# Planner priorities for weight splits and norms, and gamma folded into the opening's split

## The chip, the cores and the metric

The kernel runs on one NeuronCore of one Trainium2 chip. The metric is the device time of one execution in microseconds (us). Engines are named as in the profile: PE is the matmul engine, PEld its weight loads, DVE the vector engine, ACT the scalar engine, POOL is GpSimd, SP issues most DMAs.

## The reference, cut to what matters

Two layers work on x, 256 tokens by 1024 channels, all in float32. Cut to the parts that the change touches:

```python
for l in range(DEPTH):                               # DEPTH = 2
    h = rmsnorm(x, norm_mix[l])
    aq, ak, av, iq, ik, iw, hq, hf, hi, hg, ga, gb = split(h @ w_in[l])   # D_IN = 5956 columns
    y_attn = dsa_attention(aq, ak, av, iq, ik, iw)   # indexer scores, top 64 keys, softmax
    y_hgrn = hgrn2(hq, hf, hi) * silu(hg)            # gated linear recurrence
    merged = sigmoid(ga) * (y_attn @ w_proj_attn[l]) + sigmoid(gb) * (y_hgrn @ w_proj_hgrn[l])
    x = x + merged @ w_out[l]
    h = rmsnorm(x, norm_ffn[l])
    g, u = split(h @ w_ffn_in[l])
    x = x + (silu(g) * u) @ w_ffn_out[l]
```

## The kernel before, in words

**Arithmetic.** Each float32 matmul is made of three matmuls in the fp32r type: an operand is split into a rounded part `hi` and the rest `lo`, and `mm3` adds hi\*hi, hi\*lo and lo\*hi into one PSUM bank. Activations are the stationary side (128x128), weights the moving side (up to 512 columns). Tokens come in NT = 2 tiles of 128 (index `i`).

**Weights.** `take()` brings the next chunk of weights: SP issues the DMA into a tile `w`, ACT writes `hi` (a rounded copy), DVE writes `lo = w - hi`. There are three slots each for `hi` and `lo`. A usual chunk has 128x2048 elements and feeds 24 pairs or more of matmul and weight load; the eight chunks of the first layer's `idx` and `aq` are smaller (128x648 and 128x1024), because those groups are cut in four. `group()` runs one column group over all chunks and both token tiles; the order of groups in a layer is idx, aq, ak, hf, hq, av, vh, hg, then the gates ga, gb, ga, gb. After these come pj (the two projections), wo, fi (feed-forward in) and fo (feed-forward out). The accumulators of groups lie in four PSUM banks with tag `P`, transposes and small products in four with tag `Q`.

**Between the matmuls.** The indexer result goes through ropes and the top-64 search (`work`: pairs of MAX8 and MATCH_REPLACE8 on DVE), aq and ak through a norm and ropes, then softmax; hf and hq are copied out by ACT (`hfraw`, `hqraw`), transposed on PE (`hfp`, `hqp`) and go into the recurrence. Temporaries of these steps share six slots with tag `s2`.

**Order.** Nothing is ordered by hand. Every operation is recorded in a `Program`, and a planner (`schedule`, `path_tails`, `run`) fixes the order on each engine before anything is emitted. An operation has a cost in planner nanoseconds and a `tail`: the longest way from its start to the end, along what needs its result, along the chain of all matmul groups that are marked main, and along who reuses its slots (that hop costs `slack` more). The cost of an operation that is neither main nor on SP is multiplied by `stretch` in that sum, so work beside PE is treated as more urgent than its bare length says. On each engine the planner takes, of the operations that could start first, the one with the largest `tail + rank`. `rank` is a number in nanoseconds that the kernel may set around some operations.

```python
    def path_tails(self, stretch, slack):
        for o in reversed(self.ops):
            after = [s.tail + self.latency(o, s) for s in o.succs] + [s.tail + slack for s in o.soft]
            if o in self.next_main:
                after.append(self.next_main[o].tail)
            o.tail = (o.cost if o.main or o.eng == "SP" else o.cost * stretch) + max(after, default=0.0)
```

**The opening.** 28 small bfloat16 matmuls on zeros (`gate`, WARM of them) have a rank of -1e9 and fill PE while nothing else can run. The four blocks of x (two token tiles by two halves of 512 channels) are loaded, transposed on PE into a bank `xT`, multiplied by the norm weight gamma on DVE into `xg` (gamma lies by channel in `gcol`), rounded by ACT to `hT_hi`, and `hT_lo = xg - hT_hi` is made by DVE for the first block and by POOL for the other three.

**Norms at the end of a block.** `out_gemm` (wo and fo) finishes its two token tiles and two halves one after another; each half is added into x by DVE, multiplied by gamma, transposed, and split (`norm_half`).

All operations go through one recorded call, so nearly every row of the profile has the line L467; rows are told apart by the names of the tiles.

Of the kernel before, what the change touches and what calls it, by code (L numbers as in the profile page):

```python
# [9 lines left out]
F32 = mybir.dt.float32  # L10
# [3 lines left out]
AF = mybir.ActivationFunctionType  # L14
ALU = mybir.AluOpType
# [11 lines left out]
N_IDX = 324  # L27
C_HQ, C_HF, C_HV, C_HG, C_GA, C_GB = 1860, 2372, 2884, 3396, 3908, 4932
FIRST = {(0, C_IDX): 2, (0, C_AQ): 2}
WARM = 28  # L30
LEVELS = (2, 4, 8)
TWO_PI = 2.0 * np.pi

# [120 lines left out]
class Program:  # L154
# [298 lines left out]
    def emit(self, tc):  # L453
        nc = tc.nc
        engines = {"DVE": nc.vector, "ACT": nc.scalar, "PE": nc.tensor, "SP": nc.sync, "POOL": nc.gpsimd}
        with ExitStack() as ctx:
# [15 lines left out]
BASE, ORIGIN = 16512, 24576  # L472
SLOTS = {"w": 3, "hi": 3, "lo": 3, "hT": 8, "s4": 14, "s2": 6, "sm": 14, "work": 2, "bias": 2, "rqs": 4,
         "gbc": 2, "P": 4, "Q": 4}
TUNING = {"stretch": 1.5, "bonus": 3000.0, "slack": 4000.0}


def hybrid_trunk(prog, x_d, pos_d, w_in, w_pa, w_ph, w_out, n_mix, n_ffn,
                 q_norm, k_norm, h_norm, h_lb, w_fi, w_fo, invf_d, cf_d, cm_d, out_d):
    V, S, PE, SP, POOL = prog.vector, prog.scalar, prog.tensor, prog.sync, prog.gpsimd  # L480

    def const(name, shape, dt=F32):
        prog.add_tag("c_" + name, 1)
        return prog.tile("c_" + name, shape, dt, name)
# [4 lines left out]
    def tmp(name, shape, dt=F32):  # L489
        return prog.tile("s2", shape, dt, name)  # L490
# [4 lines left out]
    def bank(name, tag="Q"):  # L495
        return prog.tile(tag, [512], F32, name)
# [21 lines left out]
                                     for o in (0, DFF)]) + ([4, 512],))  # L518
        add_rows(w_fo, l, 2, 1024, 0)

    state = {"used": 0}

    def take():
        c = state["used"]
        state["used"] += 1
        a, b, kn = chunks[c]
        k, n = kn or b
        wt, ht, lt = "w" if k * n > 1024 else "s4", "hi", "lo"
        w = prog.tile(wt, [k, n], F32, f"w{c}")
        hi = prog.tile(ht, [k, n], F32R, f"hi{c}")  # L530
        lo = prog.tile(lt, [k, n], F32R, f"lo{c}")
        prog.rank = 5e5 - 1e3 * c
        if kn is None:
            SP.dma_start(w, a)
        else:
            SP.dma_start(w[:, :, 0:256], a)
            SP.dma_start(w[:, :, 256:512], b)
        prog.rank = 0.0
        S.activation(hi, w, AF.Copy)
        V.tensor_tensor(lo, w, hi.bitcast(F32), op=ALU.subtract)  # L540
        return hi, lo

    def mm3(acc, h, hk, wc, wk, wsl, start, stop):

        hh, hl = h
        wh, wl = wc
        with prog.one(main=True):
            PE.matmul(acc, hh[:, hk, :], wh[:, wk, wsl], start=start, stop=False)
            PE.matmul(acc, hh[:, hk, :], wl[:, wk, wsl], start=False, stop=False)
            PE.matmul(acc, hl[:, hk, :], wh[:, wk, wsl], start=False, stop=stop)  # L550
# [19 lines left out]
    V.memset(zero, 0.0)  # L570
    prog.rank = 2e6
    grow = tmp("grow", [128])
    S.dma_start(ident, cf_d[:, 0:128])
    S.dma_start(grow[0:8, :], n_mix[0].rearrange("(k d) -> k d", k=8))
    for g in range(2):
        for i in range(NT):
            prog.rank = (2e6, 499500.0)[g + i > 0] - 1e3 * (2 * g + i - 1)
            gs = slice(g * 512, (g + 1) * 512)
            SP.dma_start(x[:, i, gs], x_d[0, i * 128:(i + 1) * 128, gs])
    prog.rank = 0.0  # L580
# [2 lines left out]
    gate = bank("gate")  # L583
    for _ in range(WARM):
        PE.matmul(gate[:, 0:256], zero[:, 0:128], zero, start=True, stop=True)
# [24 lines left out]
    def transpose4(dst, src, n=4):  # L610
        with prog.one():
            for k in range(n):
                PE.transpose(dst[:, k * 128:(k + 1) * 128], src[:, k * 128:(k + 1) * 128], ident)
# [26 lines left out]
    gcol = const("gcol", [8])  # L640
    V.tensor_copy(gcol, growp[:, 0:8])
    hT = pair("hT0")
    for g in range(2):
        ks = slice(g * 4, g * 4 + 4)
        for i in range(NT):
            pt = bank(f"xT{i}{g}", "P")
            transpose4(pt, x[:, i, g * 512:(g + 1) * 512])
            xg = tmp(f"xg{i}{g}", [4, 128])
            V.tensor_tensor(xg, pt.rearrange("p (k t) -> p k t", k=4), gcol[:, ks, None].to_broadcast([128, 4, 128]), op=ALU.mult)
            first_hi = S.activation(hT[i][0][:, ks, :], xg, AF.Copy)  # L650
            E = V if g == 0 and i == 0 else POOL
            E.tensor_tensor(hT[i][1][:, ks, :], xg, hT[i][0][:, ks, :].bitcast(F32), op=ALU.subtract)
    R = []
    for i in range(NT):
        ssq = small(f"ss{i}")
# [97 lines left out]
    def layer(l, hT, R):  # L753
        last = l == DEPTH - 1
        def group(n, name, evac, kk=4):
            accs = [bank(f"{name}{i}_{l}", "P") for i in range(NT)]
            for c in range(8 // kk):
                wc = take()
                for i in range(NT):
                    for k in range(kk):  # L760
                        kt = c * kk + k
                        mm3(accs[i][:, :n], hT[i], kt, wc, k, slice(0, n), kt == 0, kt == 7)
            for i in range(NT):
                evac(i, accs[i][:, :n])
# [52 lines left out]
        def ev_qk(a, dstT):  # L817
            def ev(i, acc):
                raw = tmp(f"raw{a}{i}", [512])
                S.activation(raw, acc, AF.Copy, scale=R[i][:, 0:1])  # L820
                sq = tmp(f"sq{a}{i}", [512])
                S.activation(sq, raw, AF.Square)
                s8 = small(f"s8{a}{i}")
                V.tensor_reduce(s8[:, 0:8], sq.rearrange("p (h d) -> p h d", h=8), axis=AX.X, op=ALU.add)
                r8 = newton(s8[:, 0:8], 8, 1.0 / 64, f"n{a}{i}")
                rot = tmp(f"rot{a}{i}", [8, 64])
                rope(rot, raw.rearrange("p (h d) -> p h d", h=8), 8, rtab[l, a][0][:, i, :], rtab[l, a][1][:, i, :])
                if a == 0:
                    rqs = prog.tile("rqs", [8], F32, f"rqs{i}")
                    V.tensor_scalar(rqs, r8, 0.125, None, op0=ALU.mult)  # L830
                    rq.append(rqs)
                else:
                    V.tensor_tensor(rot, rot, r8[:, :, None].to_broadcast([128, 8, 64]), op=ALU.mult)
                pt = bank(f"qkp{a}{i}")
                transpose4(pt, rot.rearrange("p h d -> p (h d)"))
                S.activation(dstT[:, :, i * 128:(i + 1) * 128], pt.rearrange("p (k t) -> p k t", k=4), AF.Copy)
            return ev

        group(512, "aq", ev_qk(0, qT), FIRST.get((l, C_AQ), 4))
        load_g(f"f{l}", n_ffn[l])  # L840
        group(512, "ak", ev_qk(1, kT))


        PT = []
        for i in range(NT):
# [17 lines left out]
            for p in range(2):  # L863
# [4 lines left out]
                for hp in range(4):  # L868
                    h, c = 2 * hp + p, p * 4 + hp
# [4 lines left out]
                for j in range(i + 1):  # L874
                    pt = bank(f"ptp{i}{p}{j}")
# [178 lines left out]
        for i in range(NT):  # L1054
# [10 lines left out]
            pt = bank(f"yhp{i}")  # L1065
# [3 lines left out]
            split_to(yT[i][0][:, 4:8, :], yT[i][1][:, 4:8, :], pv, gc)  # L1069


        gates = {}

        def ev_gate(key):
# [11 lines left out]
        for g in range(2):  # L1086
            ws = [take(), take()]
            for i in range(NT):
# [10 lines left out]
                pt = bank(f"mp{i}", "Q")  # L1099
# [3 lines left out]
        def out_gemm(n_chunks, lhs, gkey, hT_out, name):  # L1103

            accs = [[bank(f"{name}{i}{g}", "Q") for g in range(2)] for i in range(NT)]
            for c in range(n_chunks - 2):
                wc = take()
                for i in range(NT):
                    for k in range(2):
                        (hh, hl), hk = lhs(i, 2 * c + k)  # L1110
                        with prog.one(main=True):
                            for g in range(2):
                                gs = slice(g * 512, (g + 1) * 512)
                                PE.matmul(accs[i][g], hh[:, hk, :], wc[0][:, k, gs], start=c == 0 and k == 0, stop=False)
                                PE.matmul(accs[i][g], hh[:, hk, :], wc[1][:, k, gs], start=False, stop=False)
                            for g in range(2):
                                gs = slice(g * 512, (g + 1) * 512)
                                PE.matmul(accs[i][g], hl[:, hk, :], wc[0][:, k, gs], start=False, stop=False)
            wcs = [take(), take()]
            Rn = []  # L1120
            for i in range(NT):
                ssq = small(f"{name}ss{i}")
                for g in range(2):
                    for c in range(2):
                        for k in range(2):
                            kt = 2 * (n_chunks - 2 + c) + k
                            h, hk = lhs(i, kt)
                            mm3(accs[i][g], h, hk, wcs[c], k, slice(g * 512, (g + 1) * 512), kt == 0, c == 1 and k == 1)
                    xs = x[:, i, g * 512:(g + 1) * 512]
                    V.tensor_tensor(xs, xs, accs[i][g], op=ALU.add)  # L1130
                    if hT_out is not None:
                        norm_half(i, g, gkey, hT_out, ssq, "P")
                    else:
                        SP.dma_start(out_d[0, i * 128:(i + 1) * 128, g * 512:(g + 1) * 512], xs)
                if hT_out is not None:
                    Rn.append(norm_scale(ssq, f"{name}r{i}"))
            return Rn
# [8 lines left out]
        for j in range(11):  # L1146
# [7 lines left out]
            for i in range(NT):  # L1154
                pt = bank(f"fp{j}{i}", "Q")
# [11 lines left out]
    for l in range(DEPTH):  # L1167
        hT, R = layer(l, hT, R)
# [43 lines left out]
```

## Time and profile before

| what | us |
|---|---|
| median of 3 runs | 814.75 (814.44 to 815.56) |
| the profiled execution | 815.19 |
| its span, first to last instruction | 813.4 |
| PE busy | 801.3 |
| DVE busy | 537.6 |
| ACT busy | 400.9 |
| POOL busy | 6.5 |

The profiled execution lies 0.44 us over the median; 1.8 us of it lie around the span. PE's busy time counts the drawn-out ends of pipelined matmuls, so a matmul of 512 columns is drawn with some 0.39 us although the next one starts 0.23 us after it. A stall on PE is therefore read best from the starts of two neighbouring matmuls.

### The profile page before, as it was taken

The page shows a single profiled execution, that of the slowest core. Times are in us where ns is not written, and L with a number is a line of the kernel's source. Part 1 is how long each engine was busy: PE and PEld are TensorE (multiplying, and loading weights), DVE is VectorE, ACT ScalarE, POOL GpSimd, SP SyncE. Part 2 cuts the span into 40 slices and gives each one's busy share as a digit, 9 for nine tenths or more (in the row PEclk, how much of TensorE's full clock was granted, in tenths as well). Part 3 has the DMA queues.
Part 4 walks back from the last instruction along what each step waited for, and adds up shares of the span by engine and source line. Part 5 has one row for each costly group of instructions (what it writes and reads, how often), then busy time and mean ns, then how long its engine had stood idle before and what let it go on. Part 6 is the DMA issues. An engine that isn't in the chain of part 4 may idle for free.

```text
span 813.4 us, 10251 instructions
## 1 busy us (share of the span) xinstructions
PE 801.3 (99%) x3986; PEld 657.3 (81%) x3986; DVE 537.6 (66%) x936; ACT 400.9 (49%) x506; POOL 6.5 (1%) x8
## 2 busy tenths in 40 slices
PE   8989999999999999999999999999999999999998
PEld 7767788888888888888887778888888888888886
DVE  6999856577775455554489997566868645556442
ACT  5764855344364435453356667533445544445330
POOL 3000000000000000000000000000000000000000
PEclk9998999999999999999999999999999999999999
DMA  9725555333656656536546356443354665655531
GB/s 319 248 69 176 186 188 174 104 124 129 219 176 206 195 169 203 170 144 222 168 154 219 111 201 207 155 156 105 108 202 156 206 204 168 199 177 186 169 142 52
DMA packets 86793, 139.66 MB, mean 172 GB/s; under 512 B 3269, under 2 KB 51033, under 8 KB 86745
## 3 DMA queue, kind: packets, MB, share of 16 engines
q1 hardware_dynamic: 86584, 138.94, 51.4%
q8 instruction: 31, 0.51, 0.2%
q14 instruction: 18, 0.14, 0.0%
q10 hardware_dynamic: 160, 0.07, 0.0%
HBM read 137.95 MB, written 1.05 MB: 171 GB/s over the span
## 4 chain that ended last, share of the span: by engine, by line
PE 84%; DVE 10%; issue 2%; ACT 2%; DMA 0%; POOL 0%; POOLq 0%; ACTq 0%; DVEq 0%
PE fi L467 29%; PE fo L467 15%; PE pj L467 5%; PE gb L467 5%; PE wo L467 5%; PE ga L467 4%; DVE lo L467 4%; PE av L467 3%; PE hg L467 3%; PE vh L467 3%; PE hq L467 2%; DVE work L467 2%; PE aq L467 1%; ACT hi L467 1%; PE fp L467 1%
## 5 line engine op out<-in xcount | busy, mean ns | idle before, releaser
L467 DVE TENSOR_TENSOR lo<-w,hi 128x2048 fp32r<-128x2048 f32 (+3 forms) x134 | 296.4, 2212 | 218.5 <-ACT hi L467 217.9
L467 ACT ACTIVATE hi<-w 128x2048 fp32r<-128x2048 f32 (+3 forms) x134 | 247.3, 1846 | 280.7 <-PE fi L467 95.1
L467 PE MATMUL fi<-hi,h2T_hi 128*128 128x512 f32 x352 | 140.8, 400 | 0.2
L467 PE MATMUL fi<-hi,h2T_lo 128*128 128x512 f32 x352 | 137.8, 391 | 0.0
L467 PE MATMUL fi<-lo,h2T_hi 128*128 128x512 f32 x352 | 137.1, 390 | 0.0
L467 PE MATMUL fo<-hi,act 128*128 128x512 f32 x352 | 109.9, 391 | 0.0
L467 PEld LDWEIGHTS fi<-hi,h2T_lo 128*128 128x128 f32 x352 | 66.1, 188 | 15.0 <-DVE h2T_lo L467 0.7
L467 PEld LDWEIGHTS fo<-hi,act 128*128 128x128 f32 x352 | 66.1, 188 | 13.7
L467 PEld LDWEIGHTS fi<-hi,h2T_hi 128*128 128x128 f32 x352 | 66.1, 188 | 13.3 <-DVE h2T_lo L467 0.8
L467 PEld LDWEIGHTS fi<-lo,h2T_hi 128*128 128x128 f32 x352 | 66.2, 188 | 12.6
L467 PE MATMUL fo<-lo,act 128*128 128x512 f32 x176 | 68.5, 389 | 0.0
L467 PEld LDWEIGHTS fo<-lo,act 128*128 128x128 f32 x176 | 33.1, 188 | 6.6
L467 PE MATMUL gb<-hi,hT_hi 128*128 128x512 f32 x64 | 26.7, 418 | 0.0
L467 PE MATMUL wo<-hi,mT_hi 128*128 128x512 f32 x64 | 25.9, 405 | 0.0
L467 PE MATMUL pj<-hi,yT_hi 128*128 128x512 f32 x64 | 25.8, 404 | 0.0
L467 PE MATMUL ga<-hi,hT_hi 128*128 128x512 f32 x64 | 25.7, 401 | 0.0
L467 PE MATMUL wo<-lo,mT_hi 128*128 128x512 f32 x64 | 25.1, 392 | 0.0
L467 PE MATMUL gb<-hi,hT_lo 128*128 128x512 f32 x64 | 25.1, 392 | 0.0
L467 PE MATMUL gb<-lo,hT_hi 128*128 128x512 f32 x64 | 25.0, 391 | 0.0
L467 PE MATMUL ga<-hi,hT_lo 128*128 128x512 f32 x64 | 25.0, 391 | 0.0
L467 PE MATMUL pj<-hi,yT_lo 128*128 128x512 f32 x64 | 25.0, 391 | 0.0
L467 PE MATMUL pj<-lo,yT_hi 128*128 128x512 f32 x64 | 25.0, 390 | 0.0
(340 smaller groups left out, 1302.0 us busy)
## 6 DMA issues: line engine op xcount, KB each, us to landing
w<-in_w_ffn_in_dram SPq DMA_DIRECT2D x88, 512.0 KB, 4.5
w<-in_w_in_dram SPq DMA_DIRECT2D x42, 1024.0 KB, 4.9
w<-in_w_ffn_out_dram SPq DMA_DIRECT2D x22, 1024.0 KB, 4.7
w<-in_w_out_dram SPq DMA_DIRECT2D x8, 1024.0 KB, 4.7
w<-in_w_proj_attn_dram SPq DMA_DIRECT2D x4, 1024.0 KB, 4.9
w<-in_w_proj_hgrn_dram SPq DMA_DIRECT2D x4, 1024.0 KB, 4.8
w<-in_w_in_dram SPq DMA_DIRECT2D x4, 512.0 KB, 4.6
w<-in_w_in_dram SPq DMA_DIRECT2D x4, 324.0 KB, 5.5
```

What stands on the lines that cost most here:

```text
L467: getattr(engines[o.eng], name)(*[real(x) for x in a], **{n: real(x) for n, x in k.items()})
```

## The change

Five edits. Two constants of the planner: WARM goes from 28 to 22 and `stretch` from 1.5 to 1.8. The hi and lo of a chunk get a rank: the first four chunks (idx of the first layer) one of some 3e5, interleaved with the splits of x; chunks taken from the point after the group ak to the point after hg (the groups hf, hq, av, vh, hg, in both layers) get AHEAD = 2e4; the others stay at 0. In `out_gemm` the addition into x and `norm_half` get AHEAD as well. In the opening the multiplication by gamma is part of the split: per k tile of 128 channels one ACT instruction writes `hT_hi` from PSUM with gamma as its scale, and one DVE instruction writes `hT_lo`; `xg` and POOL's part are gone. The DMA of gamma is issued ahead of that of the identity, and the ranks of the last three blocks of x fall by LATER = 6e3, so that they stand behind more of the first weight chunks on SP's queue.

```diff
-WARM = 28
+WARM = 22
+AHEAD, LATER, OPEN = 2e4, 6e3, 3e5
-TUNING = {"stretch": 1.5, "bonus": 3000.0, "slack": 4000.0}
+TUNING = {"stretch": 1.8, "bonus": 3000.0, "slack": 4000.0}
-    state = {"used": 0}
+    state = {"used": 0, "ahead": 0.0}
...
-        prog.rank = 0.0
+        prog.rank = OPEN - 1e4 * c - 5e3 if c < 4 else state["ahead"]
         S.activation(hi, w, AF.Copy)
         V.tensor_tensor(lo, w, hi.bitcast(F32), op=ALU.subtract)
+        prog.rank = 0.0
...
+    S.dma_start(grow[0:8, :], n_mix[0].rearrange("(k d) -> k d", k=8))
     S.dma_start(ident, cf_d[:, 0:128])
-    S.dma_start(grow[0:8, :], n_mix[0].rearrange("(k d) -> k d", k=8))
...
-            prog.rank = (2e6, 499500.0)[g + i > 0] - 1e3 * (2 * g + i - 1)
+            prog.rank = 2e6 if g + i == 0 else 5e5 - 1e3 * (2 * g + i - 1) - LATER
...
             pt = bank(f"xT{i}{g}", "P")
+            prog.rank = OPEN - 1e4 * (2 * g + i)
             transpose4(pt, x[:, i, g * 512:(g + 1) * 512])
-            xg = tmp(f"xg{i}{g}", [4, 128])
-            V.tensor_tensor(xg, pt.rearrange("p (k t) -> p k t", k=4), gcol[:, ks, None].to_broadcast([128, 4, 128]), op=ALU.mult)
-            first_hi = S.activation(hT[i][0][:, ks, :], xg, AF.Copy)
-            E = V if g == 0 and i == 0 else POOL
-            E.tensor_tensor(hT[i][1][:, ks, :], xg, hT[i][0][:, ks, :].bitcast(F32), op=ALU.subtract)
+            for k in range(g * 4, g * 4 + 4):
+                src = pt[:, k % 4 * 128:k % 4 * 128 + 128]
+                first_hi = S.activation(hT[i][0][:, k, :], src, AF.Copy, scale=gcol[:, k:k + 1])
+                V.scalar_tensor_tensor(hT[i][1][:, k, :], src, gcol[:, k:k + 1], hT[i][0][:, k, :].bitcast(F32),
+                                       op0=ALU.mult, op1=ALU.subtract)
+    prog.rank = 0.0
...
         group(512, "ak", ev_qk(1, kT))
+        state["ahead"] = AHEAD
...
+        state["ahead"] = 0.0
         gates = {}
...
+                    prog.rank = AHEAD
                     xs = x[:, i, g * 512:(g + 1) * 512]
                     V.tensor_tensor(xs, xs, accs[i][g], op=ALU.add)
                     if hT_out is not None:
                         norm_half(i, g, gkey, hT_out, ssq, "P")
                     else:
                         SP.dma_start(out_d[0, i * 128:(i + 1) * 128, g * 512:(g + 1) * 512], xs)
+                    prog.rank = 0.0
```

## Rows read from the trace of the kernel before

**Rows 1.** The page, part 1: engine, busy us, share of the span, xinstructions.

```profile
PE 801.3 (99%) x3986; PEld 657.3 (81%) x3986; DVE 537.6 (66%) x936; ACT 400.9 (49%) x506; POOL 6.5 (1%) x8
```

**Rows 2.** Busy time by stretch: length, PE, PEld, DVE, ACT, POOL, clock, DMA.

```profile
0.00:20.00 20.00, 17.03 (x102) 14.22 (x103) 12.58 (x25) 12.15 (x21) 6.52 (x8) 1.00 0.90 318
...
16.00:30.00 14.00, 13.84 (x67) 11.31 (x66) 13.58 (x65) 10.66 (x14) 0.29 (x1) 1.00 0.81 292
45.00:58.00 13.00, 10.84 (x52) 8.31 (x50) 13.00 (x51) 7.45 (x9) 0.00 (x0) 1.00 0.25 81
59.70:66.50 6.80, 6.18 (x15) 4.83 (x16) 6.80 (x34) 1.78 (x4) 0.00 (x0) 0.50 0.47 154
450.00:470.00 20.00, 19.50 (x94) 15.25 (x94) 20.00 (x73) 12.65 (x14) 0.00 (x0) 1.00 0.47 156
```

**Rows 3.** Waits of PE: us in total, times, longest us.

```profile
PE hq L467 <- DVE lo L467: 1.7, 3, 1.3
PE idx L467 <- POOL hT_lo L467: 1.1, 2, 0.7
```

**Rows 4.** Timeline of PE, 55 to 67 us: start us, duration us, instruction.

```profile
55.18 0.39 PE L467 MATMUL hf<-hi,hT_lo 128*128 128x512 f32 x1
55.41 0.60 PE L467 MATMUL hfp<-ident,hfraw 128*128 128x128 f32 x4
58.16 0.66 PE L467 MATMUL hfp<-ident,hfraw 128*128 128x128 f32 x4 [2.14 <-ACT hfraw L467]
58.57 0.47 PE L467 MATMUL hq<-hi,hT_hi 128*128 128x512 f32 x1
60.32 0.79 PE L467 MATMUL hq<-lo,hT_hi 128*128 128x512 f32 x1 [1.28 <-DVE lo L467]
...
66.46 0.44 PE L467 MATMUL hq<-hi,hT_hi 128*128 128x512 f32 x1
```

**Rows 5.** Timeline of DVE, 46 to 61 us, the two lo of the stretch.

```profile
46.91 2.27 DVE L467 TENSOR_TENSOR lo<-w,hi 128x2048 fp32r<-128x2048 f32 x1
...
57.98 2.29 DVE L467 TENSOR_TENSOR lo<-w,hi 128x2048 fp32r<-128x2048 f32 x1
```

**Rows 6.** Timeline of ACT, 43 to 59 us, two instructions.

```profile
43.25 1.92 ACT L467 ACTIVATE hi<-w 128x2048 fp32r<-128x2048 f32 x1 [0.76 <-PE ak L467]
...
57.43 0.67 ACT L467 ACTIVATE hfraw<-hf,r1y 128x512 f32<-128x512 f32 x1
```

**Rows 7.** Timeline of PE, second layer, 465 to 466 us.

```profile
465.12 0.48 PE L467 MATMUL hq<-hi,hT_hi 128*128 128x512 f32 x1
465.87 0.50 PE L467 MATMUL hq<-lo,hT_hi 128*128 128x512 f32 x1 [0.26 <-DVE lo L467]
```

**Rows 8.** Timeline of PE, opening: the first idx matmul, and ak.

```profile
8.27 0.39 PE L467 MATMUL idx<-hi,hT_hi 128*128 128x324 f32 x1
...
26.00 0.48 PE L467 MATMUL ak<-hi,hT_hi 128*128 128x512 f32 x1
26.64 0.51 PE L467 MATMUL ak<-lo,hT_hi 128*128 128x512 f32 x1 [0.16 <-DVE lo L467]
```

**Rows 9.** Timeline of DVE, opening: two lo of idx chunks, and xg.

```profile
8.47 1.63 DVE L467 TENSOR_TENSOR lo<-w,hi 128x648 fp32r<-128x648 f32 x1 [0.20 <-ACT hi L467]
10.02 1.27 DVE L467 TENSOR_TENSOR xg<-xT,gcol 128x512 f32<-128x512 f32 x2
11.22 0.82 DVE L467 TENSOR_TENSOR lo<-w,hi 128x648 fp32r<-128x648 f32 x1
```

**Rows 10.** Groups by shape: xcount, busy us, mean ns, then idle before.

```profile
L467 ACT ACTIVATE hsq<-po 128x128 f32<-128x128 f32 x16 | 4.2, 278 | 4.2 <-PE po L467 4.2
L467 DVE SCALAR_TENSOR_TENSOR yh<-po,hn0y,sg 128x128 f32<-128x128 f32 x4 | 1.1, 344 | 0.0
```

**Rows 11.** Timeline of PE, first feed-forward matmuls of the first layer.

```profile
229.15 0.50 PE L467 MATMUL fi<-hi,h2T_lo 128*128 128x512 f32 x1
229.74 0.50 PE L467 MATMUL fi<-hi,h2T_hi 128*128 128x512 f32 x1
```

More of the change, by code (lines that the diff above doesn't have):

```diff
@@ L643, in hybrid_trunk @@
     for g in range(2):
-        ks = slice(g * 4, g * 4 + 4)
         for i in range(NT):
             pt = bank(f"xT{i}{g}", "P")
+            prog.rank = OPEN - 1e4 * (2 * g + i)
             transpose4(pt, x[:, i, g * 512:(g + 1) * 512])
-            xg = tmp(f"xg{i}{g}", [4, 128])
-            V.tensor_tensor(xg, pt.rearrange("p (k t) -> p k t", k=4), gcol[:, ks, None].to_broadcast([128, 4, 128]), op=ALU.mult)
-            first_hi = S.activation(hT[i][0][:, ks, :], xg, AF.Copy)
-            E = V if g == 0 and i == 0 else POOL
-            E.tensor_tensor(hT[i][1][:, ks, :], xg, hT[i][0][:, ks, :].bitcast(F32), op=ALU.subtract)
+            for k in range(g * 4, g * 4 + 4):
[4 more added lines that the diff above has]
+    prog.rank = 0.0
     R = []
```

## The prediction, on record before the changed kernel was run

> **What bounds the kernel now.** I read the page's first part first: PE is busy 801.3 of 813.4 us [rows 1], so a change of order alone can win only what PE idles or runs slowly; it removes no matmul of the main chain. The next view is the starts of PE's instructions, since drawn ends hide stalls. Two neighbouring 512-column matmuls start 0.23 us apart (55.18 to 55.41) and four transposes take (0.60 - 0.27) / 3 = 0.11 us each [rows 4]. Measured against these paces, one place stands out, the passage from hf to hq in the first layer. The transposes hfp start at 55.41, the second four only at 58.16; hq's first matmul starts at 58.57, its second at 60.32, waiting for a lo [rows 4]. After that the granted clock is 0.50 from 59.7 to 66.5 us, the lower of the two levels, 1.2 GHz [rows 2]: PE had done little for 5 us, and then pays double for each matmul until it is back.
>
> Why is that lo late? The windows show DVE with 13.00 of 13.00 us busy [rows 2]. Its hi came from ACT at 43.25 + 1.92 = 45.2 us [rows 6], but the lo ran from 57.98 to 60.27 [rows 5]: nearly 13 us behind ropes, norms and the top-64 search. So it is an order on a full DVE, not a late DMA and not a lack of DVE over the whole kernel, of which it is busy for 66% [rows 1]. The second layer has the same passage with a smaller wait [rows 3, 7]. PE's list of waits has none for a lo of the gates, the projections or the feed-forward, so there no order of splits can win.
>
> **The change, part by part.** *Splits of hf to hg at AHEAD.* Raised by 20 us of planner time, the lo of hq can follow its hi: at 45.2 instead of 57.98. PE then goes on from hf to hq, and hq's matmuls also cover the late copy hfraw (ACT, 57.43 to 58.10 [rows 6]), because the second transposes can come after some of them. From 55.41 to 66.46 pass 11.05 us, with 8 transposes and 15 matmuls (hq at 58.57 and 14 from 60.32 on; the window's x15 counts the one at 66.46 for that at 58.57 [rows 2, 4]). At the full pace that is 8 x 0.11 + 15 x 0.23 = 4.3 us, so 6.7 us go: 2.3 before 58.16, 1.5 before 60.32, and 2.9 of slow clock. The bounds are 3.8 (idle gone, the clock still falls) and 6.7; I take 6.7, since with no idle there nothing is left that is like what came before the fall. In the second layer the three waits of hq for lo sum to 1.7 with a longest of 1.3 [rows 3], which leaves 0.4 for two; by starts one of them is 465.87 - 465.12 - 0.23 = 0.5 [rows 7]. Bounds 0.4 and 1.0; I take 0.9.
>
> What is behind the moved lo on DVE? At most three of 2.29 us run earlier, so ropes, norms and search come 6.9 us later. Next late are the six s2 slots, and through them hfraw, whose copy must empty a P bank before av's matmuls. Before, hfraw is out at 58.1; 6.9 later is 65.0. PE would now reach av at 55.4 + 0.9 + 48 x 0.23 = 67.3. The cover is 2.3 us, so I price this at zero; without cover it is the second rival. SP's loads profit, as w tiles come free with their lo. The two matching hi on ACT pass copies of accumulators by 1.9 us each, covered by the 11 us between a group's end and the reuse of its bank.
>
> *The opening.* Removed are four xg (1.27 for two [rows 9], 2.5 in all) and one lo on DVE, some 0.7 more, and three subtractions on POOL, for which PE waited 1.1 us [rows 3]. Added are 16 scalar_tensor_tensor on DVE. The nearest row, four of 128x128 from PSUM with a column scalar, takes 1.1 us [rows 10]: 4.4 in all, so DVE gains 1.2 us of work. It gets most of that back: the lo at 8.47 took 1.63 us beside POOL's subtraction, the one at 11.22 0.82 [rows 9]. ACT gets 16 pieces in place of four 512-wide ones; at the 278 ns of the nearest row, without a scale, that is 4.4 us [rows 10], and with 7.8 of the first 20 us idle on ACT [rows 2] even half as much again is covered, on its idle and not on the path.
>
> Cutting 512-wide operations in four is what the Trainium skill warns of (VectorE: DVE Perf Modes, "The TRN2 errata — SBUF-src ops pay a fixed extra latency per instruction"): each instruction pays a fixed latency, so pieces should have at least 512 elements. Its table, 120 cycles plus the width at 0.96 GHz from PSUM, makes an estimate of 16 x 0.26 = 4.1 us where the row makes 4.4. By the page DVE would lose 0.9 us here, by the row 1.2.
>
> What it wins is latency. The first idx matmul, at 8.27 [rows 8], need no longer wait for a whole 512-wide product, hi and lo (some 0.64 each, as xg [rows 9]), only for two pieces of 0.28: up to 1.3 us. With POOL's 1.1 the upper bound is a gain of 2.4. The lower bound is a loss: SP now issues early weights ahead of x's last blocks; a 512 KB chunk at 292 GB/s [rows 2] is 1.8 us, and if idx waits for x that long, it is lost. What is won must also survive the next splits: DVE is busy 13.58 of 14 us from 16 to 30, and the lo of ak is just in time, or 26.64 - 26.00 - 0.23 = 0.4 late [rows 2, 8]. I take a gain of 0.8, a third of the upper bound, for that reason. Six fewer warm-up matmuls and gamma's DMA ahead of the identity's I price at nothing: the first ones still run while x loads, and the rest only fill. The opening's range pays if they don't.
>
> *Norms at AHEAD.* PE waits 229.74 - 229.15 - 0.23 = 0.36 us for h2T_lo [rows 11], once in each layer: bounds 0 and 0.7, taken 0.4, since add, transposes and split must still follow one another.
>
> *Stretch 1.8.* It lifts all work beside PE against the splits that get no rank: aq, ak, gates, feed-forward. Where PE never waits for a lo I charge nothing; the cover there is the three slots of hi and lo, which let a split run two chunks ahead, some 11 us of matmuls. In the opening, aq and ak have next to none; the nearest row is the 0.4 of ak [rows 8], and I charge that once more, a loss of 0.4; bounds are 0 and one whole lo, 2.3.
>
> Sum: 6.7 + 0.9 + 0.8 + 0.4 - 0.4 = 8.4 us. The profiled execution's span goes from 813.4 to 805.0 and its time from 815.19 to 806.8; the median, 0.44 lower, to 806.3.
>
> **The rivals.** *The rank doesn't reach.* Stretch goes up by 0.3 of a helper's cost, so a chain with 20 / 0.3 = 67 us of work beside PE still ahead of it rises as much as the splits do, and the order stays. For it: search, softmax and recurrence are long. Against it: the lo lost by 13 us only, and the matmuls in between count unstretched. The two hq terms fall away, and 0.8 remains: 814.0.
>
> *The wait moves (slower).* The delayed ropes hold s2 slots, hfraw comes after 67.3, and PE waits for a P bank at av. It decides when the copies slip by more than the 9.2 us from 58.1 to 67.3 (the 6.9 above plus 2.3). Then an idle of up to 4.6 us, as much as two lo, and the clock's 2.9 come back: 7.5 in each layer, where DVE is as full (20.00 of 20.00 [rows 2]). Layer one: 7.5 - 6.7 = 0.8; layer two: 7.5 - 0.9 = 6.6; with 0.8 won elsewhere, 814.75 + 6.6 = 821.4. For it: six slots, a DVE without gaps. Against it: the cover.
>
> *The opening loses.* x comes 1.8 us late and one lo of aq or ak slips by 2.3 more, in place of a net gain of 0.4: 806.3 + 4.5 = 810.8. For it: the loads are the limit there. Against it: idx can work on the first token tile meanwhile.
>
> **How the numbers follow.** The forecast has 0.66 (803.5 to 809.5: all terms at their upper ends give 814.75 - 6.7 - 1.0 - 2.4 - 0.7 = 804.0, half a us is for smaller stalls; the upper end is the clock's 2.9 not won), the opening's loss 0.12, the rank that doesn't reach 0.12, the moved wait 0.10. The range 803.5 to 814.0 holds the first two and the better part of the third. Within 0.2%, 813.1 to 816.4, is what measurement can't tell from no change: 0.12. Faster is 0.78, slower 0.10.
>
> **What would show it.** Right: no idle of PE between hf and hq, the clock at 1.00 from 55 to 70 us, the lo of hq on DVE right after its hi, search and ropes later; the wait for POOL gone and the first idx matmul before 8.27. Wrong: a gap of PE before av with hfraw as its releaser, a lo of aq or ak that PE waits for by over 1 us, or lo of hq still behind the search.

## The result, and the profile after

The changed kernel takes 804.39 us (median of 4 runs, 803.62 to 804.76) against 814.88 for the kernel before beside it: ratio 0.9869, interval 0.9852 to 0.9886, a gain of 10.5 us. Forecast were 806.3 in 803.5 to 814.0. The profiled execution took 804.76 us, its span is 803.0.

Part 1 of the page after, beside [rows 1]:

```profile
PE 796.7 (99%) x3980; PEld 656.7 (82%) x3980; DVE 537.6 (67%) x947; ACT 407.6 (51%) x522; POOL 0.7 (0%) x5
```

DVE does as much as before, ACT 6.7 us more, POOL next to nothing. The first table to make is where PE stood at the same point of its program. The starts are read from PE's timeline in both kernels:

| stretch of PE's program | before | after | difference |
|---|---|---|---|
| start to the first hf of layer 0 | 43.05 | 43.42 | +0.38 |
| hf to pj, layer 0 | 132.15 | 124.56 | -7.59 |
| pj of layer 0 to hf of layer 1 | 271.15 | 270.52 | -0.63 |
| hf to pj, layer 1 | 126.15 | 123.91 | -2.24 |
| pj of layer 1 to the end | 240.90 | 240.56 | -0.34 |

So most came from the passages that the prediction named, and the opening gave nothing in this profiled execution. Busy time by stretch after (length, PE, PEld, DVE, ACT, POOL, clock, DMA), to lay beside [rows 2]:

```profile
43.00:55.00 12.00, 12.00 (x56) 9.94 (x55) 11.88 (x38) 5.86 (x7) 0.00 (x0) 1.00 0.43 145
55.00:70.00 15.00, 14.94 (x68) 12.07 (x67) 15.00 (x46) 8.70 (x8) 0.00 (x0) 1.00 0.63 208
59.70:66.50 6.80, 6.80 (x33) 5.61 (x33) 6.80 (x20) 3.12 (x4) 0.00 (x0) 1.00 0.48 154
```

From 59.7 to 66.5 us PE now starts 33 instructions at a granted clock of 1.00, where it started 15 at 0.50. DVE is as full as it was; only its order changed. The waits of PE after (total, times, longest), beside [rows 3]:

```profile
PE gate L468 <- DVE zero L468: 1.1, 1, 1.1
PE xT L468 <- DMA ident<-in_cf_dram: 0.5, 1, 0.5
PE aq L468 <- DVE lo L468: 0.4, 1, 0.4
PE idx L468 <- DVE lo L468: 0.3, 1, 0.3
```

The wait of hq for lo and that of idx for POOL are gone. So are those of fi (read by starts, [rows 11]) and of the recurrence, whose product hl waited twice in the kernel before:

```profile
PE hl L467 <- DVE A L467: 0.7, 2, 0.4
```

The passage from hf to hq in PE's timeline after, beside [rows 4]:

```profile
54.55 0.39 PE L468 MATMUL hf<-hi,hT_lo 128*128 128x512 f32 x1
54.77 0.39 PE L468 MATMUL hq<-hi,hT_hi 128*128 128x512 f32 x1
55.00 0.39 PE L468 MATMUL hq<-lo,hT_hi 128*128 128x512 f32 x1
```

hq follows hf 0.22 us later, and the transposes hfp have moved behind hq, to 89.6 us. The split that made it possible, in the timelines of ACT and DVE after, beside [rows 5, 6]:

```profile
43.62 1.92 ACT L468 ACTIVATE hi<-w 128x2048 fp32r<-128x2048 f32 x1 [0.32 <-PE ak L468]
...
45.57 2.29 DVE L468 TENSOR_TENSOR lo<-w,hi 128x2048 fp32r<-128x2048 f32 x1
...
51.53 2.29 DVE L468 TENSOR_TENSOR lo<-w,hi 128x2048 fp32r<-128x2048 f32 x1
```

The hi ends at 45.54 and its lo starts at 45.57, in the middle of the search; before, a lo in the same place came 13 us behind its hi.

### The profile page after: what moved, and what is told of

Same layout as the page of the kernel before. It is cut to its first block, busy times and chain, and to the rows that moved or that the text cites. A ratio compares the mean times of both kernels' runs of the same rounds, so it can differ in the third digit from the quotient of the medians.

```text
span 803.0 us, 10263 instructions
## 1 busy us (share of the span) xinstructions
PE 796.7 (99%) x3980; PEld 656.7 (82%) x3980; DVE 537.6 (67%) x947; ACT 407.6 (51%) x522; POOL 0.7 (0%) x5
## 4 chain that ended last, share of the span: by engine, by line
PE 94%; DVE 3%; DMA 2%; ACT 0%; issue 0%; SPq 0%
PE fi L468 30%; PE fo L468 15%; PE gb L468 6%; PE ga L468 5%; PE wo L468 5%; PE pj L468 5%; PE ak L468 3%; PE vh L468 3%; PE hg L468 3%; PE aq L468 3%; PE av L468 2%; PE hf L468 1%; PE hq L468 1%; DVE lo L468 1%; PE hl L468 1%; DMA w<-in_w_in_dram 1%
## 5 line engine op out<-in xcount | busy, mean ns | idle before, releaser
L468 PE MATMUL ga<-lo,hT_hi 128*128 128x512 f32 x64 | 25.0, 391 | 0.0
```

Source lines behind the costliest of these rows:

```text
L468: getattr(engines[o.eng], name)(*[real(x) for x in a], **{n: real(x) for n, x in k.items()})
```

## The experiments

All twelve kernels ran five rounds beside the kernel before. The differences are in us against the changed kernel's 804.39, which was measured in another sitting: the kernel before stood at 814.88 beside it and at 814.78 to 815.02 beside these twelve, so a difference of 0.2 says nothing.

| kernel | median (range) | ratio to before, interval | difference |
|---|---|---|---|
| e1, splits without rank | 809.73 (808.63 to 809.99) | 0.9934 [0.9921, 0.9946] | +5.34 |
| e2, rank on splits alone | 807.48 (807.36 to 808.18) | 0.9911 [0.9898, 0.9925] | +3.09 |
| e3, stretch 1.5 | 805.42 (805.06 to 805.50) | 0.9883 [0.9868, 0.9898] | +1.03 |
| e4, old opening | 805.24 (804.96 to 805.70) | 0.9883 [0.9869, 0.9896] | +0.85 |
| e5, rank from the start | 803.38 (803.26 to 803.49) | 0.9857 [0.9842, 0.9872] | -1.01 |
| e6, five s2 slots | 807.06 (806.04 to 807.54) | 0.9902 [0.9885, 0.9918] | +2.67 |
| e7, norms without rank | 805.76 (805.42 to 806.34) | 0.9887 [0.9872, 0.9902] | +1.37 |
| e8, x not behind weights | 804.46 (804.21 to 804.52) | 0.9870 [0.9855, 0.9885] | +0.07 |
| e9, stretch alone | 815.13 (814.54 to 815.85) | 1.0000 [0.9991, 1.0009] | +10.74 |
| e10, PE kept busy | 815.66 (815.17 to 816.74) | 1.0010 [1.0001, 1.0019] | +11.27 |
| e11, e5 and LATER 0 | 804.17 (803.90 to 804.42) | 0.9867 [0.9853, 0.9880] | -0.22 |
| e12, e5 and WARM 48 | 813.60 (813.33 to 816.81) | 0.9993 [0.9984, 1.0002] | +9.21 |

**The rank of the splits, taken away and given alone.** e1 is the changed kernel without the line that sets the rank behind ak:

```diff
         group(512, "ak", ev_qk(1, kT))
-        state["ahead"] = AHEAD
```

> The changed kernel, only that the chunks of hf to hg have rank 0 again (stretch 1.8, the new opening and the rank on norms stay). If the rank on splits carries the gain, the lo of hq falls behind the search again, and further than before since stretch 1.8 lifts the search: PE idles between hf and hq by 3.8 us or more in the first layer, the granted clock falls to 0.50 there, and the time is 811 to 816 us. If stretch 1.8 carries it (helpers done earlier leave DVE free for lo), PE has no such gap and the time stays at 804 to 806.

It lies between the two expectations, at 809.73. Rows of its PE timeline, and a window:

```profile
50.98 0.63 PE L468 MATMUL qkp<-ident,rot 128*128 128x128 f32 x4 [1.65 <-DVE rot L468]
...
53.48 0.50 PE L468 MATMUL hf<-lo,hT_hi 128*128 128x512 f32 x1 [1.65 <-DVE lo L468]
...
61.07 0.50 PE L468 MATMUL hq<-lo,hT_hi 128*128 128x512 f32 x1 [1.39 <-DVE lo L468]
```

```profile
55.00:70.00 15.00, 13.62 (x75) 10.63 (x74) 15.00 (x65) 8.88 (x10) 0.00 (x0) 1.00 0.40 137
```

By starts (each row's start less that of the matmul before it, less the usual pace) the three stalls are 1.81, 1.90 and 1.64: 5.35, the whole difference of 5.34. There is no clock term in this profile, whose clock stayed at 1.00; the other four runs of e1, with mean clocks of 0.995 to 0.998 over the span, had a fall. e2 does the opposite and adds only the rank to the kernel before:

```diff
+        prog.rank = state["ahead"]
         S.activation(hi, w, AF.Copy)
         V.tensor_tensor(lo, w, hi.bitcast(F32), op=ALU.subtract)
+        prog.rank = 0.0
...
         group(512, "ak", ev_qk(1, kT))
+        state["ahead"] = AHEAD
...
+        state["ahead"] = 0.0
         gates = {}
```

> The kernel before, with the rank of 2e4 on the splits of hf to hg as its only change (stretch 1.5, old opening, no rank on norms). If the rank on splits carries the gain: the gap at hq and the fall of the clock are gone, and PE is 7 to 9 us ahead of the kernel before at the gates of the second layer: 805.5 to 808. If it needs stretch 1.8 too: 811 or more. The waits of the recurrence for DVE near 149 and 547 us (0.5 each before) should then still be there.

As expected, 807.48: 7.4 us under the 814.85 of before beside it. The gap before hq is gone, and what the other edits remove is still in its list of waits:

```profile
PE idx L468 <- POOL hT_lo L468: 1.0, 2, 0.7
...
PE hl L468 <- DVE F L468: 0.4, 1, 0.4
PE hl L468 <- DVE A L468: 0.4, 1, 0.4
```

**Stretch.** e3 sets it back to 1.5, e9 raises it to 1.8 in the kernel before and changes nothing else.

```diff
-TUNING = {"stretch": 1.8, "bonus": 3000.0, "slack": 4000.0}
+TUNING = {"stretch": 1.5, "bonus": 3000.0, "slack": 4000.0}
```

> The changed kernel with stretch 1.5 again. If stretch is only a side part: 804 to 806, with the two waits of the recurrence for DVE (0.5 us each) back, so some 1 us over the changed kernel if these came off by stretch and by nothing else. If stretch carries the gain: 811 or more. If the ranks of 2e4 lift the splits further at stretch 1.5, the copies hfraw come later still, and PE waits for a P bank at av by more than the 0.2 us that the changed kernel shows there.

> The kernel before with one number changed: stretch 1.8 in place of 1.5, no rank anywhere, the old opening. Theory A (what was measured against the full change holds alone too): the kernel without rank on the splits was at 809.73, and it also has the new opening (0.85) and the norms' rank (1.4); taking these away gives 809.7 + 2.2 = 811.9 us, 811 to 813, with the two waits of the recurrence's hl gone, a PE stall of some 3 us left between hf and hq, and a granted clock that stays at 1.00 behind it. Theory B (the prediction's sign: a larger stretch alone makes the lo of aq and ak later and costs 0.4): 815.2 us, 814.5 to 817, with the clock at 0.50 from about 60 to 66.5 us.

e3 loses 1.0 and has two waits of the recurrence's product hl again, by starts 0.80 at 141.91 and 0.53 at 537.25 us. So beside the ranks the larger stretch gains 1.0. Alone it gains nothing: e9 is at 815.13, the number of its theory B, but not for B's reason. The lo of aq and ak are as late as before; it is hf's lo that slipped. Its PE and DVE timelines, and two windows:

```profile
49.87 0.39 PE L467 MATMUL hf<-hi,hT_hi 128*128 128x512 f32 x1
53.62 0.50 PE L467 MATMUL hf<-lo,hT_hi 128*128 128x512 f32 x1 [3.36 <-DVE lo L467]
...
51.28 2.29 DVE L467 TENSOR_TENSOR lo<-w,hi 128x2048 fp32r<-128x2048 f32 x1
```

```profile
50.00:54.00 4.00, 0.64 (x4) 0.30 (x2) 4.00 (x7) 2.43 (x2) 0.00 (x0) 1.00 0.00 0
55.00:59.00 4.00, 4.00 (x12) 3.10 (x12) 4.00 (x20) 0.95 (x2) 0.00 (x0) 0.59 0.70 252
```

The search, made more urgent, goes ahead of the split; PE stalls for 3.5 us and the clock falls. hl's waits are gone in e9 too, and from hf to pj in layer 0 its profile is 2.2 us shorter than that of before. It loses this again: 0.9 up to hf, 0.5 in layer 1 with its two waits for lo (1.0 and 1.3 by starts), and 0.8 in the rest, where no stall shows it. That the larger stretch needs a rank on the splits beside it is not shown: e1 has none and is still 5.1 us under before, of which the opening and the norms by their own runs below are 2.2. Why e1 shows no wait in layer 1 is not explained.

**The clock.** The prediction put 2.9 us on the granted clock of 0.50 [rows 2]. e10 is the kernel before in its own order; only the transposes hfp of layer 0 are written out again and again, so that PE works through the stall:

```diff
-                for name, a, k in o.calls:
+                for name, a, k in o.calls * getattr(o, "again", 1):
...
+            if l == 0 and name == "hf":
+                prog.ops[-1].again = (6, 4)[i]
```

> The kernel before in its own order on every engine, only that the transposes hfp of the first layer are written out six times (first token tile) and four times (second), so that PE works through the stall between hf and hq without doing anything useful; the stall's 3.8 us stay, filled. Theory A (the fall of the granted clock from 59.7 to 66.5 us follows from PE having little to do from 55.4 to 60.3, and costs 2.9): clock 1.00 throughout 55 to 70, 814.9 - 2.9 = 812.0 us, 811.5 to 812.7. Theory B (the fall has another cause, or costs nothing that is not given back): 814.3 to 815.5 us. If the clock is 1.00 in this kernel's trace and the time is still about 814.9, the fall in the profiled execution of before was not in its timed runs, and the 2.9 never were to be won.

PE, DVE and a window of e10:

```profile
55.88 4.71 PE L467 MATMUL hfp<-ident,hfraw 128*128 128x128 f32 x40
60.34 0.48 PE L467 MATMUL hq<-hi,hT_hi 128*128 128x512 f32 x1
61.96 0.50 PE L467 MATMUL hq<-lo,hT_hi 128*128 128x512 f32 x1 [1.14 <-DVE lo L467]
...
69.03 0.50 PE L467 MATMUL hq<-lo,hT_hi 128*128 128x512 f32 x1 [1.31 <-DVE lo L467]
...
58.77 0.42 DVE L467 TENSOR_TENSOR ropet<-raw,rs 128x256 f32<-128x256 f32 x1 [1.07 <-PE hfp L467]
```

```profile
55.00:70.00 15.00, 12.55 (x75) 10.12 (x74) 13.93 (x53) 8.03 (x9) 0.00 (x0) 1.00 0.21 70
```

The clock stays at 1.00, so it did fall because PE had little to do. But nothing is won: 815.66, just above the range of theory B. The reason is the next lo. In the kernel before, DVE and then PE:

```profile
65.04 2.29 DVE L467 TENSOR_TENSOR lo<-w,hi 128x2048 fp32r<-128x2048 f32 x1
...
68.81 0.39 PE L467 MATMUL hq<-lo,hT_hi 128*128 128x512 f32 x1
```

There the lo ends at 67.33 and PE, slow, takes it at 68.81, 1.48 us later. At full clock PE would have stood before it, and in e10 it does, at 69.03. So of the 2.9 at most 1.5 could be won while the lo come as they do. e10's own lo come later, since the added transposes hold DVE up by 1.07 us. Counted from hf's first matmul (43.05 before, 43.48 in e10), the lo of the rows above lands 1.2 us later in e10, and yet PE reaches av's first matmul after 33.28 us before and 33.27 in e10. So over this passage the clock made good what the late lo cost. Of the 0.9 by which e10's median lies above before's, 0.4 stands ahead of hf in its profile; the rest isn't located. Its third expectation, that the fall might be missing from the timed runs, falls: the mean granted clock over the whole span is 0.996 to 0.998 in all 27 runs of before listed beside e10, and 0.999 or 1.000 in all 11 of e10.

The timed runs give a second measure, since a lower mean clock is a longer fall. Of those 27 runs, the 13 at 0.996 have a median of 815.23, the 11 at 0.997 one of 814.64 and the 3 at 0.998 one of 814.35. The kernel before's runs beside the other experiments lie the same way, and in e12 the three runs at 0.996 are the slowest (815.39 to 816.81, the others 813.33 to 814.36). In e1 it doesn't show: its one run at 1.000 is the slowest, 809.99. So in the kernel before a longer fall goes with 0.6 to 0.9 us more; that the fall is the cause of it is likely and not shown.

**The opening.** e4 is the changed kernel with the opening of before, its 28 warm-up matmuls, its ranks and its order of DMAs; cut to its core:

```diff
-WARM = 22
+WARM = 28
...
-            for k in range(g * 4, g * 4 + 4):
...
+            V.tensor_tensor(xg, pt.rearrange("p (k t) -> p k t", k=4), gcol[:, ks, None].to_broadcast([128, 4, 128]), op=ALU.mult)
+            first_hi = S.activation(hT[i][0][:, ks, :], xg, AF.Copy)
+            E = V if g == 0 and i == 0 else POOL
+            E.tensor_tensor(hT[i][1][:, ks, :], xg, hT[i][0][:, ks, :].bitcast(F32), op=ALU.subtract)
```

> The changed kernel with the opening of the kernel before (gamma into xg, POOL's subtractions, the old order of DMAs, 28 warm-up matmuls, rank 0 on the first four chunks). The trace of the changed kernel has PE 0.4 us later than before at the end of idx and ak, with its clock rising at 10.4 us and not at 5.1. So by the trace this kernel is as fast or some 0.4 us faster: 803.5 to 804.4, with the clock up near 5 us and the waits for POOL (1.1 us) back. By my prediction (the new opening wins 0.8) it would be 805.2.

At 805.24 the opening is worth 0.85, though the profiled execution showed +0.38 at hf. What misled is in PE's timeline, after and then e7, which has the same opening:

```profile
7.61 1.06 PE L468 MATMUL xT<-ident,x 128*128 128x128 f32 x4
8.32 0.62 PE L468 MATMUL idx<-hi,hT_hi 128*128 128x324 f32 x1
8.74 0.47 PE L468 MATMUL idx<-lo,hT_hi 128*128 128x324 f32 x1
9.01 0.47 PE L468 MATMUL idx<-hi,hT_lo 128*128 128x324 f32 x1
...
10.83 0.31 PE L468 MATMUL idx<-lo,hT_hi 128*128 128x324 f32 x1
10.98 0.31 PE L468 MATMUL idx<-hi,hT_lo 128*128 128x324 f32 x1
```

```profile
8.06 0.40 PE L468 MATMUL idx<-hi,hT_hi 128*128 128x324 f32 x1
8.30 0.31 PE L468 MATMUL idx<-lo,hT_hi 128*128 128x324 f32 x1
8.44 0.31 PE L468 MATMUL idx<-hi,hT_lo 128*128 128x324 f32 x1
```

Matmuls of 324 columns follow one another after 0.27 us until about 10 us in the one execution and after 0.15 from the start in the other, nearly two to one; aq's first matmul comes at 18.03 and 17.20. So a single profile can't price an opening here; the medians can. Where the 0.85 lies, the stalls by starts show in part: e4 waits 0.69 and 0.84 for POOL and 0.42 for a lo of ak, the changed kernel 0.46 for a lo of idx and 0.59 for one of aq, 0.9 less in all. e4 takes all parts of the opening back together, so what the warm-up matmuls, the ranks or the split are worth alone is not shown. One part changed nothing: in both traces ACT's queue issues the identity's DMA at 0.73 us and gamma's behind it, at 1.17 before and 1.18 after. The first idx matmul is no earlier than in [rows 8]: the transposes of the next block of x stand ahead of it on PE. In e7's execution it came at 8.06, so this sign changes with the execution too.

e8 and e11 leave x where it was on SP's queue, in the changed kernel and in e5:

```diff
-AHEAD, LATER, OPEN = 2e4, 6e3, 3e5
+AHEAD, LATER, OPEN = 2e4, 0.0, 3e5
```

> The changed kernel with LATER = 0, so that x's last three blocks keep the DMA ranks of the kernel before and stand ahead of more of the first weight chunks. If the place of x on the queue delays idx: idx ends earlier than the 17.9 us of the changed kernel, by up to 1.8, and the time is 803 to 804. If the opening gains from w first (as the diff has it): the first idx matmul is later than 8.3 us and the time 804.5 to 805.5. The time at which the granted clock rises (10.4, 10.0 and 9.5 us in the three traces with the new opening, 5.1, 4.6 and 3.9 in those with the old) tells whether the order of the loads has to do with it.

> The changed kernel with all ranks of chunks at 2e4 from the start (803.38 alone) and LATER at 0, so that x is not put behind weights. Theory A (the order of x's loads is hidden by the weight chunks that idx works through, as it was without the early rank, 804.46 against 804.39): 803.4 us, 802.9 to 803.9. Theory B (with lo of aq no longer late, x is what the opening waits for): 802.4 to 802.9.

In the changed kernel this is worth nothing (804.46). With the early rank it costs 0.8 (804.17 against 803.38), which neither theory of e11 had: idx starts at 9.65 in place of 7.44 there, and its last matmul at 17.51 in place of 16.65. In e8 idx starts late too, at 9.97, and its last matmul still starts at 17.76, against 17.88 in the changed kernel. So by the medians x behind the first weights is the better order once the rank is early; why only then is not shown. e8's question on the clock has an answer: the first record of 1.00 in the trace comes at 10.4 us in the changed kernel and at 4.2 in e7, whose openings are the same, and at 10.5 in e9 with the old one. So the order of the loads does not fix it.

**The norms.** e7 leaves their rank out:

```diff
-                    prog.rank = AHEAD
                     xs = x[:, i, g * 512:(g + 1) * 512]
```

> The changed kernel without the rank on the addition into x and the norms after it. If that rank is what removed PE's two waits of 0.37 us for h2T_lo at the start of fi: they come back, and 805.1 to 805.4 (0.7 to 1.0 more). If stretch 1.8 lifts these operations enough by itself: 804.4 within 0.4, no wait at fi.

It loses 1.37. Three stalls return, by starts 0.37 at 221.76, 0.34 at 409.70 and 0.37 at 617.36; the first of them in PE's timeline, beside [rows 11]:

```profile
221.16 0.50 PE L468 MATMUL fi<-hi,h2T_lo 128*128 128x512 f32 x1
221.76 0.50 PE L468 MATMUL fi<-hi,h2T_hi 128*128 128x512 f32 x1
```

They sum to 1.08; the other 0.3 isn't located.

**The slots s2.** e6 takes one of the six away to bring the second rival about.

```diff
-SLOTS = {"w": 3, "hi": 3, "lo": 3, "hT": 8, "s4": 14, "s2": 6, "sm": 14, "work": 2, "bias": 2, "rqs": 4,
+SLOTS = {"w": 3, "hi": 3, "lo": 3, "hT": 8, "s4": 14, "s2": 5, "sm": 14, "work": 2, "bias": 2, "rqs": 4,
```

> The changed kernel with five s2 slots for temporaries in place of six. This takes away cover of the copies hfraw and hqraw, as in my second rival. In the changed kernel hfraw for the second token tile is out at 68.9 us, with PE at av from 66.2 on, and PE waits 0.2 us at av for hqraw: no cover is left there, where I had counted 2.3 us. If the slots set the time of these copies, PE idles at av by 1 to 5 us in the first layer, perhaps with a fall of the clock: 805.5 to 812. If the copies are late for another reason (their place in ACT's order), there is no change: 804.4 within 0.5.

It loses 2.67, but elsewhere: PE waits 2.46 at 20.37 us for a lo of aq, and there is no wait for a P bank at av. The planner made another order of the whole stretch, so the run says nothing of that rival.

**A better version, and one worse.** e5 starts with the rank instead of setting it behind ak, so that the later chunks of idx, aq and ak have it too; e12 has 48 warm-up matmuls in addition.

```diff
-    state = {"used": 0, "ahead": 0.0}
+    state = {"used": 0, "ahead": AHEAD}
```

```diff
-WARM = 22
+WARM = 48
```

> The changed kernel, with the rank of 2e4 also on the splits of aq and ak in the first layer (the rank holds from the first chunk on; the first four keep theirs). In the changed kernel PE waits 0.46 us for the lo of the last idx chunk and 0.59 us for that of the first aq chunk; ACT does two sums of squares ahead of that aq hi. If the missing rank at stretch 1.8 is what makes these late, the second wait goes, PE is 0.5 to 1 us earlier at hf, and the time is 803.4 to 803.9. If the opening is bound by loads and by x, the waits stay and the time is 804.4; if it delays the norms of the opening and with them the idx copies, a wait of PE shows near 27 to 35 us and it is slower.

> The changed kernel with all ranks of chunks at 2e4 from the start (803.38 alone) and 48 warm-up matmuls in place of 22. Theory A (the granted clock rises at another time in each execution of the same opening, so more warm-up changes nothing that can be seen): 803.4 us, 802.9 to 804.0. Theory B (more warm-up brings the clock up before the first idx matmul in every execution): idx from 8.3 to 10.1 us runs at a pitch of 0.15 in place of 0.27, up to 0.8 less: 802.6 us, with a record of 1.00 from about 4 us on. Theory C (warm-up matmuls hold a Q bank and PE while x's transposes could start): 804 to 805 with the first idx matmul later than 8.5.

e5 is the fastest of all at 803.38; hf starts at 40.52 in place of 43.42 us, and 1.0 of that reaches the end. The time is as expected, but the waits did not go: by starts PE still waits 0.47 for a lo of idx and 0.53 for one of aq. e12 is none of its three theories. DVE and PE of e12:

```profile
40.55 2.29 DVE L468 TENSOR_TENSOR lo<-w,hi 128x2048 fp32r<-128x2048 f32 x1 [1.32 <-ACT hi L468]
45.99 2.29 DVE L468 TENSOR_TENSOR lo<-w,hi 128x2048 fp32r<-128x2048 f32 x1 [3.15 <-ACT hi L468]
51.43 2.29 DVE L468 TENSOR_TENSOR lo<-w,hi 128x2048 fp32r<-128x2048 f32 x1 [3.14 <-ACT hi L468]
53.64 0.48 DVE L468 TENSOR_TENSOR idr<-idxraw,IC 128x320 f32<-128x320 f32 x1
...
49.29 2.58 PE L468 MATMUL gate<-zero 128*128 128x256 bf16 x22
54.79 0.52 PE L468 MATMUL idp<-ident,idr 128*128 128x128 f32 x3 [2.93 <-DVE idr L468]
```

The opening did get faster (the last idx matmul starts at 15.96 against 16.65 in e5), but 22 of the 48 were left over, fill PE only at 49.29 and hold their Q bank until then. The indexer's ropes (idr) stand on DVE behind four splits, and DVE idles 3 us before each of two of these, for a hi that waits for hf on PE. Search and softmax start late, and 10 us are lost. That the bank is what put the ropes there is not shown, and the kernel before speaks against it: its last warm-up matmul too comes at 49.00, and its idr starts at 29.37. Why the planner put the ropes so late in e12 stays open.

## Why the prediction was right, and where it was not

**Place and mechanism held.** The lo of hq follows its hi, PE goes from hf to hq without a gap, the clock is 1.00 from 55 to 70 us, and POOL's wait is gone, as the prediction's last part asked. The gain is 2.1 over the 8.4 of the sum; the norms (1.0 more) and stretch (1.4 more) account for it, by their own runs. Taken by their runs, the terms stand so:

| term | forecast | measured |
|---|---|---|
| splits at AHEAD, both layers | -7.6 | -7.4 alone (e2), -5.3 as the last edit (e1) |
| opening | -0.8 | -0.85 (e4) |
| norms | -0.4 (0 to 0.7) | -1.4 (e7) |
| stretch 1.8 | +0.4 (0 to 2.3) | -1.0 beside the rest (e3), 0 alone (e9) |

With e2 for the splits these sum to 10.7, and 10.5 were measured; with e1 they would sum to 8.6. The edits work on one another, so no such sum is a division of the gain.

**The splits: the sum right, one part of it wrong.** The passage of layer 0 gave 7.6 where 6.7 was forecast; the difference is a wait of hl behind it (0.52 by starts, at 149.42 us of before) and one of the transposes qkp ahead of it (0.33, at 53.56). But only a part of the 2.9 charged to the clock was the clock's own price. In the kernel before, PE ran slowly toward a lo that was itself late: up to 1.5 by the clock, the rest by that lo, as the rows of before beside e10 show. Moving the splits takes both away, so the sum came out; a step that had cured the clock alone would have won at most 1.5. The lower bound of 3.8 (idle gone, clock still falling) rested on the same error. Layer 1 gave 2.2 against 0.9: the two waits of hq were 0.43 and 0.51 by starts, as forecast, and 0.5 is hl again, which is the stretch's. 0.4 is no gain: four transposes qkp stand ahead of hf after and behind it before (436.67 and 447.72 us), which moves them into the stretch ahead. The rest lies in gaps of 0.1 between hq's matmuls.

**The norms: two waits counted, three there.** The step read fi's wait in each layer [rows 11] and missed the first aq of layer 1, which waits 0.34 for its lo in the same stretch of DVE. The upper bound of 0.7 was therefore no bound.

**Stretch: the wrong side was looked at.** I asked only what a stronger urgency beside PE would delay. What it hastens is the recurrence, for whose product hl PE waited twice, 0.5 each, in the kernel before. The price I feared exists. In e9 it falls on hf and hq. Beside the ranks it falls on idx and aq: the changed kernel waits 0.46 and 0.59 for a lo there, e3 with stretch 1.5 only 0.41, so 0.6 where 0.4 was charged. The gain at hl is the larger one.

**The opening: the size right, one sign of it missing.** The pieces cost what [rows 10] promised, 4.4 us for each engine. Groups by shape after:

```profile
L468 ACT ACTIVATE hT_hi<-xT,gcol 128x128 fp32r<-128x128 f32 x16 | 4.8, 371 | 2.2 <-PE xT L468 1.3 <-DVE hT_lo L468 0.8
...
L468 DVE SCALAR_TENSOR_TENSOR hT_lo<-xT,gcol,hT_hi 128x128 fp32r<-128x128 f32 x16 | 4.7, 346 | 2.4 <-ACT hT_hi L468 2.4
```

That is 4.8 for ACT and 4.7 for DVE. But the first idx matmul was to come before 8.27 and started at 8.32 in the profile, with the transposes of the next block of x ahead of it; 8.06 in e7 shows that the sign could not decide. The gain lies behind, where POOL's waits were. The lower bound took a chunk of 512 KB for what is issued ahead of x; the first four are idx's, of 324 KB, so that at the same rate it is 1.1 us and not 1.8.

**The rivals.** That the rank doesn't reach is out. That the wait moves came nearer than I counted. ACT and then PE after:

```profile
60.41 0.69 ACT L468 ACTIVATE hfraw<-hf,r0y 128x512 f32<-128x512 f32 x1 [2.44 <-DVE rot L468]
...
68.18 0.67 ACT L468 ACTIVATE hfraw<-hf,r1y 128x512 f32<-128x512 f32 x1
69.03 0.69 ACT L468 ACTIVATE hqraw<-hq,r0y 128x512 f32<-128x512 f32 x1 [0.18 <-DVE rot L468]
...
66.16 0.39 PE L468 MATMUL av<-hi,hT_hi 128*128 128x512 f32 x1
...
69.33 0.39 PE L468 MATMUL av<-hi,hT_lo 128*128 128x512 f32 x1
69.78 0.50 PE L468 MATMUL av<-hi,hT_hi 128*128 128x512 f32 x1
```

The second hfraw is out at 68.85, 10.8 us after the 58.10 of before, where I allowed 6.9 and said that a slip of over 9.2 decides. So the rival's condition was met, and PE reached av at 66.16, even before the 67.3 of the sum. What did not come was its price: PE is 0.2 us late at 69.78, just behind the end of hqraw at 69.72, and not up to 4.6. The first hfraw was out at 61.10, and PE had 15 matmuls of av to start before it had to wait. The prediction didn't count that cover, so that the rival cost so little is in part luck, and 0.10 was too low for it; e12 shows what it is like when work beside PE does come too late. One figure of the chances doesn't follow: the upper end of the forecast, 809.5, is called the clock's 2.9 not won, which from 806.3 gives 809.2.

## What to carry to other kernels

On a full engine, look for an operand that was ready long before it was used: moving splits of 2.3 us ahead of up to 13 us of search won 7 us without removing an instruction. When PE is slow ahead of a wait, ask when the next operand lands before charging the slow pace: a clock cured ahead of a late operand wins no more than the time up to that operand, here 1.5 of 2.9 us. Price an edit of a planner's weights by what it hastens as well as by what it delays, and measure it beside the edits it comes with, since here the same number won 1.0 with the other edits and nothing alone.

## What the runs showed of the hardware

The same opening ran its first six idx matmuls at 0.27 us a piece in one execution and at 0.15 in another. The windows print a clock of 1.00 for both, so there the pitch of the rows is what shows it. The Trainium skill (TensorE: Matmul & The Clock Gate, "What's actually happening") says that how many matmuls run slow at the start of a kernel differs from run to run; these traces agree.

The clock fell to 0.50, the lower level of 1.2 GHz, in the profiles of before, e9 and e12, each time after PE had done little: busy for 1.10 us from 55.8 to 59.7 in before, 0.64 from 50 to 54 in e9, 0.21 from 52 to 55 in e12. It did not fall in the profile of e1, whose 5.3 us of stalls are split by matmuls, and did in that kernel's other four runs by their mean clocks (0.995 to 0.998).

A lo of 648 columns took 1.63 us beside POOL's subtraction [rows 9]; after, all four take 0.82 or 0.83. In e4, with POOL back, a lo that starts at 8.63 while POOL's subtraction runs from 8.04 to 9.53 takes 1.59 again: 0.90 until POOL ends and 0.69 more. The Trainium skill (SBUF — State Buffer, "SBUF: two separate sides") says that a DVE operation with two inputs in SBUF and a GpSimd operation that reads SBUF shut each other out for a whole instruction; the rows agree roughly, the rest after POOL's end being 0.13 shorter than a lo alone.
